# Output projection of a hybrid decoder layer: pools in another order, row statistics behind three accumulations, norms one tile later

## The chip, the core and the metric

One core of a Trainium2 chip runs the whole layer as one program. The metric is the device time of one execution in microseconds (us). TensorE is called PE, its weight loads PEld, VectorE DVE, ScalarE ACT, GpSimd POOL; SP is the queue that issues nearly all DMAs.

## What is computed

The reference, cut to the part that matters. `oa` and `ob` are the outputs of two groups of attention heads, 2048 positions by 512 columns each.

```python
mixed = jnp.concatenate([rmsnorm(oa, g_out_a[l]), rmsnorm(ob, g_out_b[l])], axis=-1)
x = x + jnp.einsum('bse,ed->bsd', mixed, w_o[l])
h = rmsnorm(x, g_ffn[l])
act = jax.nn.silu(jnp.einsum('bsd,df->bsf', h, w_gate[l])) * jnp.einsum('bsd,df->bsf', h, w_up[l])
x = x + jnp.einsum('bsf,fd->bsd', act, w_down[l])
return rmsnorm(x, g_final)
```

`rmsnorm(x, g)` divides each row by the root of its mean square and multiplies by `g`. `w_o` is 1024 by 1024, `w_gate` and `w_up` are 1024 by 2816, `w_down` is 2816 by 1024; all is float32. The layer before this part makes the input projection (`project`) and the two attentions (`MixerA`, `attend_b`).

## The kernel before

A float32 product is made of three matmuls of rounded operands: high by high, high by low, low by high. So each operand is split into a high half (a cast on ACT) and a low half (a subtraction on DVE or POOL), and a product over 512 columns of contraction takes 12 matmuls of 128x512.

**The projection** is `project_out`, lines 802 to 924. The 2048 rows are four tiles `t` of 512, and the contraction is two groups `g` of 512: `g` 0 for `oa`, 1 for `ob`. One call of `add(t, g)` (line 909) does one tile and one group:

- `prep_o` (833) loads four chunks of attention output (`ob`, 512 KB each, in two parts that are added at line 848) with their denominators `fb` (847), multiplies them (850 or 854, result `os_`), splits the result into the halves of `oT` (856 on ACT, 857 on DVE) and sums the squares over the four chunks (860 on ACT, 864 on DVE) into one buffer, `sacc`.
- Four matmuls of one column with a vector of ones (867, `pss`; a profile shows them as eight instructions) turn the squares into a sum per row; `rstd_of` (106) makes the reciprocal root of it: one DVE instruction (`ms_o`, 108) and one POOL power (`rs_o`, 110).
- `load_x` (827) fetches the tile's x into `xs`, with `g` 0 only.
- `outproj` (870) makes eight accumulations of 12 matmuls (881), 96 matmuls in all, and adds each to `xs` on DVE, scaled by `rs` (885, the eviction). On its first call for a group it loads and splits the weights `wo` (`load_wo`, 816; loads 821, casts 823, subtractions 824 on DVE for group 0 and on POOL for group 1).

`norm2(t)` (887) stores a finished tile (893), squares it on ACT (895), scales it in place on DVE (897), transposes it with 32 matmuls on PE (902), copies the transposes to `hst` on ACT (903) and stores them in DRAM as `hT` (905). `ffn_in` (927) loads `hT` of two tiles at a time again (`hraw`, 950), makes seven operands of it per chunk (A11, S2, S1, S3, A12, A22, S4; lines 953 to 972) and seven split weights (`wh`, `wl`, 977 and 979), and starts with `first_quads` (1043), whose first matmul is line 1050.

**What sets the order.** Python writes the program in the order of the calls, and a scheduler with a model of the machine then merges it into one list per engine and queue. Each engine runs its list in order. The calls are: `add(0,0)`, `add(1,0)`, `add(0,1)`, then for t = 1 to 3 `norm2(t-1)`, `add(t,1)`, `add(t+1,0)`, and `norm2(3)`.

**Buffers.** PSUM has eight banks, all in the pool `ps` with the one tag `mm`: accumulations, `pss` and transposes share them. SBUF pools are stacked from the foot in the order in which they are opened (lines 809 to 811, after `rw3` with its four load buffers of 16 KB together, sizes per partition): `c3` 4 KB (`gf`, the row of g_ffn), `s3` some 4, `op` 20, `wo30` 32, `slot` 48 (six buffers of `oT`, three groups), `x3` 32 (two tiles of `xs`), `hst` 16, `wo31` 32. Before this phase the same room belongs to the attention's pools, and after it to those of `ffn_in`: `g3` 12, `t3` 28, `a3` 112 (the operands, in the order of the list above, high half then low half), `whl3` 36 (the split weights). A tile waits for whatever used its room before (`reuse_waits="tile"`).

Of the kernel before, what the change touches and what calls it, by code (L numbers as in the profile page):

```python
# [13 lines left out]
ALU = mybir.AluOpType  # L14
# [11 lines left out]
NT = S // 512  # L26
# [79 lines left out]
def rstd_of(nc, pool, ss, n, width, half, name, bufs=2):  # L106
    ms = pool.tile([P, width], F32, tag="ms", name="ms_" + name, bufs=bufs)
    nc.vector.tensor_scalar(out=ms, in0=ss, scalar1=1.0 / n, scalar2=EPS, op0=ALU.mult, op1=ALU.add)  # L108
    rs = pool.tile([P, width], F32, tag="rs", name="rs_" + name, bufs=bufs)
    nc.gpsimd.tensor_tensor(out=rs, in0=ms, in1=half[:, :width], op=ALU.pow)  # L110
    return rs


def bcast_row(nc, dst, row):
    nc.sync.dma_start(dst, row.partition_broadcast(P))
# [669 lines left out]
def phase3(tc, consts, x, w_o, g_ffn, w_gate, w_up, w_down, g_final, out, sc):  # L785
    nc = tc.nc
    with ExitStack() as es:
        ps = es.enter_context(tc.tile_pool(name="ps3", bufs=8, space=PSUM, reuse_waits="tile"))
        rw = es.enter_context(tc.tile_pool(name="rw3", bufs=4, reuse_waits="tile"))
        project_out(tc, consts, ps, rw, x, w_o, g_ffn, sc)  # L790
        ffn_in(tc, ps, rw, w_gate, w_up, sc)
        ffn_out(tc, consts, ps, rw, w_down, g_final, out, sc)
# [9 lines left out]
def project_out(tc, consts, ps, rw, x, w_o, g_ffn, sc):  # L802

    nc = tc.nc
    ident, half, ones, gout = consts
    xr = x[0].rearrange("(i r) d -> r i d", r=16)
    wov = w_o[0].rearrange("(k p) n -> p k n", p=P)
    with ExitStack() as es:
        pool = lambda name, bufs: es.enter_context(tc.tile_pool(name=name, bufs=bufs, reuse_waits="tile"))
        cp, sp, op, wp0, slot, xp, hp, wp1 = (pool(n, b) for n, b in (  # L810
            ("c3", 1), ("s3", 2), ("op", 2), ("wo30", 1), ("slot", 6), ("x3", 2), ("hst", 2), ("wo31", 1)))
        wp = (wp0, wp1)
        gf = cp.tile([P, D], F32, name="gf")
        wo = {}

        def load_wo(g, hf):
            wh = wp[g].tile([P, 4, 512], F32R, tag=f"woh{g}{hf}", name=f"woh{g}{hf}")
            wl = wp[g].tile([P, 4, 512], F32R, tag=f"wol{g}{hf}", name=f"wol{g}{hf}")
            for u in range(2):
                raw = rw.tile([P, 2, 512], F32, tag="raw", name="wraw_o")  # L820
                nc.sync.dma_start(raw, wov[:, 4 * g + 2 * u:4 * g + 2 * u + 2, hf * 512:(hf + 1) * 512])
                ks = slice(2 * u, 2 * u + 2)
                nc.scalar.copy(wh[:, ks], raw)
                (nc.gpsimd if g else nc.vector).tensor_sub(wl[:, ks], raw, wh[:, ks].bitcast(F32))
            wo[g, hf] = (wh, wl)

        def load_x(t):
            xs = xp.tile([P, 4, D], F32, tag="xs", name=f"xs{t}")
            for i in range(4):
                nc.sync.dma_start(xs[:, i, :], xr[RES[4 * t + i]])  # L830
            return xs

        def prep_o(t, g):

            dma = nc.sync.dma_start
            oT = [slot.tile([P, 2, 2, 512], F32R, tag="slot", name="oT") for _ in range(2)]
            for k in range(4 * g, 4 * g + 4):
                ob = op.tile([P, 2, 512], F32, tag="ob", name="ob")
                os_ = op.tile([P, 512], F32, tag="os", name="os_")
                rows = slice((k % 4) * P, (k % 4 + 1) * P)  # L840
                if k < 4:
                    dma(ob, sc.oA[:, t, rows, :].rearrange("s p n -> p s n"))
                else:
                    dma(ob, sc.oB[:, rows, t * 512:(t + 1) * 512].rearrange("s p n -> p s n"))
                fb = op.tile([P, 512], F32, tag="fb", name="fb")
                for u in range(2):
                    dma(fb[u * 64:u * 64 + 64], (sc.fA[t, 2 * k + u] if k < 4 else sc.fB[k - 4, t, u]).partition_broadcast(64))
                nc.vector.tensor_add(ob[:, 0], ob[:, 0], ob[:, 1])
                if k < 4:
                    nc.vector.tensor_mul(os_.rearrange("p (r j a) -> p r j a", r=4, j=16),  # L850
                                         ob[:, 0].rearrange("p (j r a) -> p r j a", j=16, r=4),
                                         fb.rearrange("p (j r a) -> p r j a", j=16, r=4))
                else:
                    nc.vector.tensor_mul(os_, ob[:, 0], fb)
                hi, lo = oT[k % 4 // 2][:, k % 2, 0], oT[k % 4 // 2][:, k % 2, 1]
                nc.scalar.activation(hi, os_, AF.Copy, scale=gout[:, k:k + 1])
                nc.vector.scalar_tensor_tensor(lo, os_, gout[:, k:k + 1], hi.bitcast(F32),
                                               op0=ALU.mult, op1=ALU.subtract)
                sq = op.tile([P, 512], F32, tag="sq" if k % 4 else "sacc", name="sq3", bufs=1)
                nc.scalar.activation(sq, os_, AF.Square)  # L860
                if k % 4 == 0:
                    acc = sq
                else:
                    nc.vector.tensor_add(acc, acc, sq)
            pss = ps.tile([P, 4], F32, tag="mm", name="pss")
            for i in range(4):
                nc.tensor.matmul(pss[:, i:i + 1], acc[:, i * P:(i + 1) * P], ones, start=True, stop=True)
            return oT, rstd_of(nc, sp, pss, 512, 4, half, f"o{t}{g}")

        def outproj(xs, g, oT, rs):  # L870
            for hf in range(2):
                if (g, hf) not in wo:
                    load_wo(g, hf)
            for i in range(4):
                for hf in range(2):
                    wh, wl = wo[g, hf]
                    acc = ps.tile([P, 512], F32, tag="mm", name="acco")
                    n = 0
                    for kk in range(4):
                        for a, b in ((0, wh), (0, wl), (1, wh)):  # L880
                            nc.tensor.matmul(acc, oT[kk // 2][:, kk % 2, a, i * P:(i + 1) * P], b[:, kk, :],  # L881
                                             start=(n == 0), stop=(n == 11))
                            n += 1
                    xv = xs[:, i, hf * 512:(hf + 1) * 512]
                    nc.vector.scalar_tensor_tensor(xv, acc, rs[:, i:i + 1], xv, op0=ALU.mult, op1=ALU.add)

        def norm2(t, xs):
            hst = [hp.tile([P, 4, 512], F32, tag="hst", name="hst") for _ in range(2)]
            sq = sp.tile([P, D], F32, tag="sqr", name="sqr", bufs=1)
            for i in range(4):  # L890
                cols = slice(i * P, (i + 1) * P)
                h2 = xs[:, i, :]
                nc.sync.dma_start(sc.x1[t, :, i], h2)
                ss = sp.tile([P, 1], F32, tag="ssr", name="ssr")
                nc.scalar.activation(sq, h2, AF.Square, accum_out=ss)
                rs = rstd_of(nc, sp, ss, D, 1, half, f"f{t}_{i}")
                nc.vector.scalar_tensor_tensor(h2, h2, rs, gf, op0=ALU.mult, op1=ALU.mult)
                for kg in range(2):
                    pt = ps.tile([P, 4, P], F32, tag="mm", name="pt3")
                    for kk in range(4):  # L900
                        k = kg * 4 + kk
                        nc.tensor.transpose(pt[:, kk, :], h2[:, k * P:(k + 1) * P], ident)
                    nc.scalar.copy(hst[kg][:, :, cols], pt)
            for kg in range(2):
                nc.sync.dma_start(sc.hT[t, :, 4 * kg:4 * kg + 4, :], hst[kg])

        xs = {}

        def add(t, g):
            o = prep_o(t, g)  # L910
            if g == 0:
                xs[t] = load_x(t)
            outproj(xs[t], g, *o)

        add(0, 0)
        add(1, 0)
        bcast_row(nc, gf, g_ffn[0])
        add(0, 1)
        for t in range(1, NT):
            norm2(t - 1, xs[t - 1])  # L920
            add(t, 1)
            if t + 1 < NT:
                add(t + 1, 0)
        norm2(NT - 1, xs[NT - 1])


# [295 lines left out]
```

## Time and profile before

| | us |
|---|---|
| median of three runs (2484.49 to 2489.96) | 2489.6 |
| the profiled execution | 2490.19 |
| its span, first to last instruction | 2488.4 |
| PE busy in the span | 2373.2 (95%) |
| DVE, ACT, POOL busy | 1444.7, 1029.5, 457.9 |
| the projection's first and last accumulating matmul | 888.3, 1111.7 |
| mean granted TensorE clock, of full speed | 0.974 |

The span lies inside the execution's time; some 2 us are around it. Busy time of PE overlaps, as matmuls are pipelined, so a stretch is read by when instructions start and by what ended the idle time before them. The granted clock has two levels, 1.2 and 2.4 GHz; a mean between them says for how much of a stretch each was granted.

### The profile page before, as it was taken

The numbers are of one execution on the slowest core, as the hardware profiler recorded it, in microseconds if no ns is written. First come the engines' busy times: TensorE is split into PE (matmuls) and PEld (weight loads), VectorE is DVE, ScalarE is ACT, GpSimd is POOL, SyncE is SP. The second block draws the span as 40 slices with busy tenths as digits, with TensorE's granted clock in tenths as the row PEclk, the third lists the DMA queues.
The fourth block names the chain that finished last, engine by engine and source line by source line (L and its number), as shares of the span: only waits on it lengthen the run. The fifth ranks groups of instructions, "written<-read, shape, count | busy, mean of one in ns | idle before, by whom it ended". The sixth has DMA issues, their size and how long they took to land. (4 is left out here: it accounts for less than half of the span.)

```text
span 2488.4 us, 33691 instructions
## 1 busy us (share of the span) xinstructions
PE 2373.2 (95%) x12029; PEld 2016.7 (81%) x12029; DVE 1444.7 (58%) x2969; ACT 1029.5 (41%) x2361; POOL 457.9 (18%) x431
## 2 busy tenths in 40 slices
PE   7999999989999878997999999899999999999998
PEld 7987788878999767775888888688888878888886
DVE  5335544457999766659655665965566433434342
ACT  5323355454888933335323333432332232423241
POOL 2311211111111010112110110311011051414140
PEclk9999999997999988998999999999999999999999
DMA  7666666668896886724222222422222163636361
GB/s 220 209 191 204 166 187 168 154 182 209 216 224 166 217 245 218 248 103 148 93 85 78 92 85 68 134 87 85 85 85 85 64 234 131 239 119 237 123 232 60
DMA packets 250136, 384.27 MB, mean 154 GB/s; under 512 B 19680, under 2 KB 148320, under 8 KB 244464
## 3 DMA queue, kind: packets, MB, share of 16 engines
q1 hardware_dynamic: 244784, 367.03, 49.0%
q0 software_dynamic: 4896, 14.75, 1.9%
q8 instruction: 95, 1.56, 0.3%
q14 instruction: 73, 0.60, 0.1%
q10 hardware_dynamic: 288, 0.33, 0.0%
HBM read 263.43 MB, written 118.62 MB: 154 GB/s over the span
## 5 line engine op out<-in xcount | busy, mean ns | idle before, releaser
L1136 PE MATMUL dn<-wh_d,act 128*128 128x512 f32 x1408 | 434.9, 390 | 2.4 <-ACT act L1116 2.3
L1136 PEld LDWEIGHTS dn<-wh_d,act 128*128 128x128 f32 x1408 | 264.9, 188 | 58.4 <-ACT act L1116 2.7
L1127 DVE TENSOR_TENSOR wl_d<-wraw_d,wh_d 128x1024 fp32r<-128x1024 f32 x88 | 138.3, 1578 | 272.1 <-ACT wh_d L1125 272.1
L1136 PE MATMUL dn<-wl_d,act 128*128 128x512 f32 x704 | 274.4, 390 | 0.0
L1084 POOL TENSOR_TENSOR c<-c,c 128x512 f32<-128x512 f32 x66 | 104.8, 1589 | 713.5 <-DVE c L1030 524.6
L977 ACT CAST wh<-T 128x512 fp32r<-128x512 f32 x176 | 108.7, 622 | 257.3 <-PE Yg L1012 71.7
L468 DVE TENSOR_TENSOR hl<-pt,hl 128x512 fp32r<-128x512 f32 (+1 forms) x224 | 145.2, 657 | 80.2 <-ACT hl L467 79.6
L443 ACT ACTIVATE p<-t,m 128x256 f32<-128x256 f32 (+1 forms) x384 | 176.8, 477 | 25.9 <-DVE m L668 25.9
L169 PE MATMUL acc<-hh,wh 128*128 128x512 f32 x416 | 170.1, 409 | 0.7 <-DVE vt L239 0.7
L169 PE MATMUL acc<-hh,wl 128*128 128x512 f32 x416 | 170.4, 410 | 0.0
L169 PE MATMUL acc<-hl,wh 128*128 128x512 f32 x416 | 170.0, 409 | 0.0
L1117 POOL TENSOR_TENSOR act<-actr,act 128x512 fp32r<-128x512 f32 x88 | 122.7, 1414 | 256.9 <-ACT act L1116 256.8
L881 PE MATMUL acco<-woh,oT 128*128 128x512 f32 x512 | 166.2, 404 | 0.0
L1125 ACT CAST wh_d<-wraw_d 128x1024 fp32r<-128x1024 f32 x88 | 92.1, 1050 | 166.8 <-PE dn L1136 145.2
L1136 PEld LDWEIGHTS dn<-wl_d,act 128*128 128x128 f32 x704 | 132.5, 188 | 27.5
L486 PE MATMUL o<-hl,v 128*128 128x128 f32 (+1 forms) x816 | 142.5, 295 | 7.1 <-DVE hl L468 6.1
L421 PE MATMUL s<-k,q 128*128 128x256 f32 (+1 forms) x768 | 131.9, 310 | 15.9 <-DVE hl L468 7.1
L467 ACT CAST hl<-pt 128x512 fp32r<-128x512 f32 (+1 forms) x224 | 124.7, 566 | 45.5 <-PE pt L462 45.1
L979 DVE TENSOR_TENSOR wl<-T,wh 128x512 fp32r<-128x512 f32 x176 | 122.7, 701 | 32.9 <-ACT wh L977 32.6
L462 PE MATMUL pt<-ident,p 128*128 128x128 f32 x848 | 134.2, 280 | 2.4 <-ACT p L443 1.6
L421 PEld LDWEIGHTS s<-k,q 128*128 128x128 f32 x768 | 111.1, 212 | 23.2 <-DVE nma L558 7.3
L486 PEld LDWEIGHTS o<-hl,v 128*128 128x128 f32 x816 | 112.2, 194 | 11.7 <-DVE hl L468 9.6
(453 smaller groups left out, 5520.4 us busy)
## 6 DMA issues: line engine op xcount, KB each, us to landing
wraw_d<-in_w_down_dram SPq DMA_DIRECT2D x88, 512.0 KB
wraw_g<-in_w_gate_dram SPq DMA_DIRECT2D x44, 512.0 KB
wraw_u<-in_w_up_dram SPq DMA_DIRECT2D x44, 512.0 KB
actr<-actS SPq DMA_DIRECT2D x44, 512.0 KB
actS<-c SPq DMA_DIRECT2D x68, 256.0 KB
k<-kB SPq DMA_DIRECT2D x32, 512.0 KB
xt<-in_x_dram SPq DMA_DIRECT2D x16, 512.0 KB
qA<-hia SPq DMA_DIRECT2D x32, 256.0 KB
```

The lines of the kernel that those rows point to most:

```text
L169: nc.tensor.matmul(acc, a[:, k, :], mv, start=(n == 0), stop=(n == 3 * KC - 1))
L421: nc.tensor.matmul(s[:, i, :n], b["q"], b["k"][m], start=(m == 0), stop=(m == 1))
L443: nc.scalar.activation(b["pv"](p[:, i, :n]), b["tv"](b["t"]), AF.Exp, scale=-1.0, bias=nm[:, c:c + 1], accum_out=l[:, c:c + 1])
L462: nc.tensor.transpose(pt[:, sl, :], p[:, i, hfn * P:(hfn + 1) * P], ident)
L467: nc.scalar.copy(hi, pt[:, a:z, :])
L468: nc.vector.tensor_sub(lo, pt[:, a:z, :], hi.bitcast(F32))
L486: nc.tensor.matmul(out, v[:, vi, :], mov, start=(first and n == 1), stop=(last and n == 2 * len(jobs)))
L881: nc.tensor.matmul(acc, oT[kk // 2][:, kk % 2, a, i * P:(i + 1) * P], b[:, kk, :], start=(n == 0), stop=(n == 11))
L979: nc.vector.tensor_sub(lo, src, hi.bitcast(F32))
L1117: nc.gpsimd.tensor_sub(a[:, 1], raw[:, u], a[:, 0].bitcast(F32))
L1127: nc.vector.tensor_sub(wl, raw, wh.bitcast(F32))
L1136: nc.tensor.matmul(acc[i], acts[kk][:, a, i * P:(i + 1) * P], w[kk // 2][b][:, kk % 2, :], start=(kk == 0 and n == 0), stop=(kk == NF - 1 ...
```

## The change

The pools are opened in another order, `op` and `wo30` first and `c3` and `s3` last. `prep_o` returns the summed squares instead of their reciprocal root, and `outproj` makes that root after its third accumulation (`group_rstd`); the three finished accumulations are evicted then, each later one as it ends. The calls at the end now run tile by tile, each norm after the next tile's two groups.

```diff
--- before.py
+++ after.py
@@ -807,8 +807,8 @@
     wov = w_o[0].rearrange("(k p) n -> p k n", p=P)
     with ExitStack() as es:
         pool = lambda name, bufs: es.enter_context(tc.tile_pool(name=name, bufs=bufs, reuse_waits="tile"))
-        cp, sp, op, wp0, slot, xp, hp, wp1 = (pool(n, b) for n, b in (
-            ("c3", 1), ("s3", 2), ("op", 2), ("wo30", 1), ("slot", 6), ("x3", 2), ("hst", 2), ("wo31", 1)))
+        op, wp0, slot, xp, hp, wp1, cp, sp = (pool(n, b) for n, b in (
+            ("op", 2), ("wo30", 1), ("slot", 6), ("x3", 2), ("hst", 2), ("wo31", 1), ("c3", 1), ("s3", 2)))
         wp = (wp0, wp1)
         gf = cp.tile([P, D], F32, name="gf")
         wo = {}
@@ -862,15 +862,19 @@
                     acc = sq
                 else:
                     nc.vector.tensor_add(acc, acc, sq)
+            return oT, acc
+
+        def group_rstd(t, g, acc):
             pss = ps.tile([P, 4], F32, tag="mm", name="pss")
             for i in range(4):
                 nc.tensor.matmul(pss[:, i:i + 1], acc[:, i * P:(i + 1) * P], ones, start=True, stop=True)
-            return oT, rstd_of(nc, sp, pss, 512, 4, half, f"o{t}{g}")
-
-        def outproj(xs, g, oT, rs):
+            return rstd_of(nc, sp, pss, 512, 4, half, f"o{t}{g}")
+
+        def outproj(t, xs, g, oT, sq):
             for hf in range(2):
                 if (g, hf) not in wo:
                     load_wo(g, hf)
+            accs = []
             for i in range(4):
                 for hf in range(2):
                     wh, wl = wo[g, hf]
@@ -881,8 +885,14 @@
                             nc.tensor.matmul(acc, oT[kk // 2][:, kk % 2, a, i * P:(i + 1) * P], b[:, kk, :],
                                              start=(n == 0), stop=(n == 11))
                             n += 1
-                    xv = xs[:, i, hf * 512:(hf + 1) * 512]
-                    nc.vector.scalar_tensor_tensor(xv, acc, rs[:, i:i + 1], xv, op0=ALU.mult, op1=ALU.add)
+                    accs.append((i, hf, acc))
+
+                    if len(accs) == 3:
+                        rs = group_rstd(t, g, sq)
+                    if len(accs) >= 3:
+                        for i_, hf_, acc in accs if len(accs) == 3 else accs[-1:]:
+                            xv = xs[:, i_, hf_ * 512:(hf_ + 1) * 512]
+                            nc.vector.scalar_tensor_tensor(xv, acc, rs[:, i_:i_ + 1], xv, op0=ALU.mult, op1=ALU.add)
 
         def norm2(t, xs):
             hst = [hp.tile([P, 4, 512], F32, tag="hst", name="hst") for _ in range(2)]
@@ -910,17 +920,18 @@
             o = prep_o(t, g)
             if g == 0:
                 xs[t] = load_x(t)
-            outproj(xs[t], g, *o)
+            outproj(t, xs[t], g, *o)
 
         add(0, 0)
         add(1, 0)
         bcast_row(nc, gf, g_ffn[0])
         add(0, 1)
-        for t in range(1, NT):
+        add(1, 1)
+        norm2(0, xs[0])
+        for t in range(2, NT):
+            add(t, 0)
+            add(t, 1)
             norm2(t - 1, xs[t - 1])
-            add(t, 1)
-            if t + 1 < NT:
-                add(t + 1, 0)
         norm2(NT - 1, xs[NT - 1])
```

How the instruction lists change at three places:

PE at the end of the attention, before. `o` and `pf` are the last matmuls of the attention and a transpose of its denominators.

```order
L486 MATMUL o<-hl,v_1_9937 128x2x4x32 x5
L486 MATMUL o<-hl,v_1_9937 128x4x32 x2
L681 MATMUL pf<-ident,rcs 32x128
L867 MATMUL pss<-ones_83,sq_10288 128x1 x4
L881 MATMUL acco<-woh_10343,oT 128x512
L881 MATMUL acco<-wol_10344,oT 128x512
```

And now, the same place:

```order
L486 MATMUL o<-hl,v_1_9937 128x2x4x32 x5
L486 MATMUL o<-hl,v_1_9937 128x4x32 x2
L681 MATMUL pf<-ident,rcs 32x128
L885 MATMUL acco<-woh_10334,oT 128x512
L885 MATMUL acco<-wol_10335,oT 128x512
```

The sums of squares have left this place; they follow 36 matmuls later, behind the third accumulation, and so in each of the eight groups.

SP in the attention's second to last stretch, before. `wraw_o` are the weights of the projection, `gf` is g_ffn, `v_0` and `v_1` belong to the last attention head.

```order
L821 DMA wraw_o<-in_w_o_dram 128x2x512 x3
L842 DMA ob<-oA 128x2x512
L847 DMA fb<-fA 64x512 x2
L821 DMA wraw_o<-in_w_o_dram 128x2x512
L115 DMA gf<-in_g_ffn_dram 128x1024
L842 DMA ob<-oA 128x2x512
L847 DMA fb<-fA 64x512 x2
L613 DMA v_0_9935<-vR 128x16x128
L617 DMA v_1_9937<-vR 32x16x128 x3
```

And now:

```order
L821 DMA wraw_o<-in_w_o_dram 128x2x512 x3
L842 DMA ob<-oA 128x2x512
L847 DMA fb<-fA 64x512 x2
L821 DMA wraw_o<-in_w_o_dram 128x2x512
L842 DMA ob<-oA 128x2x512
L847 DMA fb<-fA 64x512 x2
L821 DMA wraw_o<-in_w_o_dram 128x2x512 x3
L613 DMA v_0_9935<-vR 128x16x128
L617 DMA v_1_9937<-vR 32x16x128 x2
```

Three loads of the second group's weights stand ahead of the last head's v, and `gf` has left. On ACT the four casts of the first group's weights (line 823) stood behind the last cast of the attention; now they stand among its exponentials, some 40 to 55 rows earlier, and the four DVE subtractions (824) with them.

ACT at the end of the phase, before. `hst` are the copies of the last tile's transposes, `wh` the first weights of the FFN.

```order
L903 COPY hst<-pt_12055 128x4x128
L903 COPY hst<-pt_12061 128x4x128
L977 CAST wh<-wraw_g 128x512
L977 CAST wh<-T_12099 128x512
L977 CAST wh<-T_12097 128x512
L977 CAST wh<-T_12109 128x512
L977 CAST wh<-wraw_g 128x512
L977 CAST wh<-T_12119 128x512
L977 CAST wh<-wraw_g 128x512
L955 CAST A11h<-hraw 128x512
```

And now:

```order
L988 CAST wh<-T_12119 128x512
L988 CAST wh<-wraw_g 128x512
L913 COPY hst<-pt_11995 128x4x128
L913 COPY hst<-pt_12015 128x4x128
L913 COPY hst<-pt_12035 128x4x128
L913 COPY hst<-pt_12055 128x4x128
L913 COPY hst<-pt_12001 128x4x128
L913 COPY hst<-pt_12021 128x4x128
L913 COPY hst<-pt_12041 128x4x128
L913 COPY hst<-pt_12061 128x4x128
L966 CAST A11h<-hraw 128x512
```

The seven weight casts stand ahead of the last tile's eight copies now. Ahead of those casts stand the eight copies of the tile before it, whose 32 transposes PE makes right before the last tile's 32.

## Rows read from the trace of the kernel before

**Rows 1.** The page's 40 slices of the span: PE busy, granted clock, in tenths.

```profile
PE   7999999989999878997999999899999999999998
PEclk9999999997999988998999999999999999999999
```

**Rows 2.** Stretches: length, busy of PE, PEld, DVE, ACT, POOL, clock, DMA share, GB/s.

```profile
836.00:842.00 6.00, 5.49 (x27) 5.30 (x27) 5.80 (x17) 2.55 (x8) 0.00 (x0) 0.50 1.05 367
876.00:894.00 18.00, 8.03 (x27) 6.43 (x26) 12.32 (x19) 6.59 (x10) 1.04 (x1) 0.62 1.00 305
...
1112.00:1130.00 18.00, 4.84 (x35) 4.20 (x34) 6.99 (x12) 10.44 (x21) 0.54 (x1) 0.68 0.45 175
```

**Rows 3.** PE in order of time: start, us, engine, line, count [idle before, what ended it].

```profile
875.42 0.80 PE L486 MATMUL o<-hl,v 128*128 128x256 f32 x5 [0.24 <-DVE hl L468]
881.79 0.37 PE L681 MATMUL pf<-ident,rcs 128*32 128x128 f32 x1 [5.57 <-DVE rcs L678]
886.56 1.87 PE L867 MATMUL pss<-ones,sq 128*128 128x1 f32 x8 [4.40 <-DVE sq L864]
...
893.70 0.40 PE L881 MATMUL acco<-wol,oT 128*128 128x512 f32 x1
...
912.32 0.39 PE L881 MATMUL acco<-woh,oT 128*128 128x512 f32 x1
917.36 1.87 PE L867 MATMUL pss<-ones,sq 128*128 128x1 f32 x8 [4.64 <-DVE sq L864]
...
924.47 0.40 PE L881 MATMUL acco<-wol,oT 128*128 128x512 f32 x1
...
943.32 0.95 PE L867 MATMUL pss<-ones,sq 128*128 128x1 f32 x8
...
966.03 1.03 PE L902 MATMUL pt<-ident,xs 128*128 128x128 f32 x8
...
985.85 0.40 PE L881 MATMUL acco<-wol,oT 128*128 128x512 f32 x1
...
1028.11 3.66 PE L902 MATMUL pt<-ident,xs 128*128 128x128 f32 x32
1037.39 1.87 PE L867 MATMUL pss<-ones,sq 128*128 128x1 f32 x8 [5.62 <-DVE xs L885]
...
1043.78 0.62 PE L881 MATMUL acco<-woh,oT 128*128 128x512 f32 x2
...
1111.97 2.78 PE L902 MATMUL pt<-ident,xs 128*128 128x128 f32 x24
...
1129.01 0.79 PE L1050 MATMUL FA<-A11h,wh 128*128 128x512 f32 x1 [10.94 <-ACT A11h L955]
```

**Rows 4.** DVE in order of time, the same columns.

```profile
877.33 1.22 DVE L824 TENSOR_TENSOR wol<-wraw_o,woh 128x1024 fp32r<-128x1024 f32 x1
...
890.51 0.69 DVE L848 TENSOR_TENSOR ob<-ob 128x512 f32<-128x512 f32 x1 [1.88 <-DMA ob<-oA]
...
907.46 3.85 DVE L848 TENSOR_TENSOR ob<-ob 128x512 f32<-128x512 f32 x1 [4.84 <-DMA ob<-oA]
...
1035.98 0.69 DVE L848 TENSOR_TENSOR ob<-ob 128x512 f32<-128x512 f32 x1 [5.15 <-DMA ob<-oB]
```

**Rows 5.** ACT in order of time, the same columns.

```profile
839.96 0.63 ACT L860 ACTIVATE sq<-os__10291 128x512 f32<-128x512 f32 x1 [2.65 <-DVE os__10291 L850]
...
874.67 3.87 ACT L823 CAST woh<-wraw_o 128x1024 fp32r<-128x1024 f32 x4
...
1029.95 3.98 ACT L903 COPY hst<-pt 128x512 f32<-128x512 f32 x8
...
1124.70 0.62 ACT L977 CAST wh<-wraw_g 128x512 fp32r<-128x512 f32 x1 [5.96 <-DMA hT<-hst]
```

**Rows 6.** SP's queue in order of time: issue of the last tile's two stores.

```profile
1118.28 0.81 SPq L905 DMA_DIRECT2D hT<-hst  x2
```

**Rows 7.** POOL in order of time, the same columns.

```profile
903.56 7.19 POOL L824 TENSOR_TENSOR wol<-wraw_o,woh 128x1024 fp32r<-128x1024 f32 x3
```

## The prediction

> **What bounds the kernel now.** I read the page's 40 slices first: TensorE (PE) is at 9 in most of them; of the few that are lower, four lie close together (62.2 us a slice): 8, 7, 8 in the 14th to 16th (809 to 995 us) and 7 in the 19th (1120 to 1182), and the granted clock is at 8 in three of these [rows 1]. That is the output projection and its two borders, and the whole change lies there. Next I read the stretches around the drops. Over 876 to 894 us PE is busy 8.03 of 18 us at a mean granted clock of 0.62, over 1112 to 1130 4.84 of 18 us at 0.68 [rows 2]. Then PE's own order of time with what ended each idle stretch [rows 3]. The reader is to see a pattern there. Matmuls of 512 columns start 0.227 us apart at the full 2.4 GHz: from 893.70 (the 14th of a group of 96) to 912.32 (the 96th) are 82 steps in 18.62 us. Every long stall is followed by matmuls and sums of squares at 1.2 GHz (eight pss matmuls take 1.87 us at 917.36, 0.95 at 943.32), until the clock comes back some 6 to 7 us after PE resumed.
>
> I price a place as the time from its last full-speed matmul to the first full-speed one after it, less the same work at full rate (0.227 us a matmul, 0.8 us the eight pss instructions, 3.7 us the 32 transposes of a tile, as at 1028.11). All from [rows 3]:
> - a, border to the attention: 876.2 (875.42 + 0.80) to 893.70 is 17.5 us; work 0.4 + 0.8 + 13 x 0.227 = 4.2; loss **13.3**.
> - b, second group: 912.55 to 924.47 is 11.9; work 0.8 + 13 x 0.227 = 3.8; loss **8.1**.
> - c, first norm: 966.03 to 985.85 is 19.8; work 3.7 + 0.8 + 10 x 0.227 = 6.8; loss **13.0**.
> - d, second norm: 1028.11 to 1043.78 is 15.7; work 3.7 + 0.8 + 11 x 0.227 = 7.0; loss **8.7**.
> - e, border to the FFN: from 1111.97 to the first FFN matmul at 1129.01 are 17.0 us, with 3.7 of transposes in them.
>
> So 43 us are lost at a to d and about 13 at e. The third and sixth to eighth groups, whose sums of squares were ready, show nothing of it: at 943.32 PE runs on.
>
> **The change part by part.**
>
> *Sums of squares behind three accumulations.* The same eight pss instructions per group, but PE no longer needs them to begin. At 886.56 and 917.36 it sat 4.40 and 4.64 us for the last sum (DVE sq); now it needs only the oT halves. The three accumulations (36 x 0.227 = 8.2 us) cover the chain of sums. If that cover is gone, the old wait returns at its old price. New waits: three PSUM banks and one for pss are held until the reciprocal root is there. Eight banks minus these four leave four accumulations, 4 x 12 x 0.227 = 10.9 us, before PE would stand. The chain is one DVE instruction, one POOL power and a DVE eviction, some 3 us when DVE is free. The single accumulator of squares is held 8.2 us longer, so the next group's third and fourth chunks are prepared behind it; 13.6 us of its group then remain for them. I cost both at nothing.
>
> *Norms between other tiles' projections.* In c and d, PE stood since a tile's norm followed its own last eviction directly: the transposes waited for ms_f and xs, and at 1037.39 for DVE evictions (5.62 us) that stood in DVE's order behind an addition waiting 5.15 us for its load [rows 4]. Now 21.8 us of another tile's group lie between. The transposes of tiles 0 and 1 find their rows ready; only the fourth row's normalisation still comes near the end, and 24 transposes (2.8 us) run ahead of it. I take c and d whole: 13.0 + 8.7 = **21.7**. Bounds: nothing, if another wait takes each place, to 21.7; I take the upper end since PE's queue holds nothing there any more that is late. What could be late next is the load of the next tile's x: it waits for these transposes, and 512 KB pieces of it share the queue with the 2 MB stores of hT. The first eviction that needs it now comes 8.2 us later than before, which covers it.
>
> *Pool order, at a.* With op and wo30 at the foot, the first weights no longer wait for the attention's late buffers. Their four ACT casts (3.87 us at 874.67) and four DVE subtractions move from behind the attention into it. Two of those subtractions, of 1.22 us each, stood before the last reciprocal, which releases pf at 881.79 [rows 3, 4]: pf comes 2.4 us sooner after the attention's end. All four stood before the last oT half. So PE would start its projection at about 880 instead of 888.4 (886.56 + 1.87), if the attention ended as now. It will not: the casts now stand among exponentials on ACT. One cast fits into the 2.65 us that ACT idled before 839.96; the other three, 0.97 us each, push a full engine by **2.9** us [rows 5]. On SP, three more 512 KB weight loads go ahead of the last head's v loads, one (g_ffn) leaves: 1.05 MB more in a queue that was full at 367 GB/s over 836 to 842 [rows 2], 2.9 us. Both delay the same stages at the same time, so I count 2.9 once (bounds 0 and 5.8). What is left of a: an idle stretch of 881.79 - 2.4 - 876.2 = 3.2, 2.9 of delay, a slow clock once more (about eleven matmuls at twice their time, 11 x 0.227 = 2.5) and, as an estimate, 0.5 of waiting for the last oT half: 9.1 of 13.3. Gain **4** (1 to 9; the upper end if the clock does not fall at all).
>
> Behind it stands a page: by the Trainium skill, DMA: Bandwidth & Descriptors (Queues, rings and completion order), descriptors on an engine are consumed in ring order. By that the v loads cannot overtake the weights, and the sum would lose another 2.9 if the two delays add.
>
> *Second group, b.* Its third chunk was late because a DVE addition at 907.46 waited for its load and then took 3.85 us, not 0.69 as at 890.51 [rows 4]. Ahead of that load now stand 2.1 MB of second-half weights fewer and 0.5 MB of g_ffn more: about 1.6 MB at 305 GB/s (876 to 894 [rows 2]), 5 us sooner, against a start 2.9 us later and a PE that asks 4.5 us earlier. I leave 1.5 us of stall: gain **6.5** (0 to 8.1).
>
> *Border e.* Let E be PE's last projection matmul. Before, FFN weight casts stood until 1124.70 for the store of hst [rows 5], since the new pools lay over hst. Now those pools lie over wo31, free at E, and the seven casts run early. But tile 2's norm moved to the end too: its eight copies (4.0 us, as at 1029.95) end about E + 6; tile 3's copies need the same two hst buffers, so they wait for that store, 6.4 us (1118.28 to 1124.70 [rows 5, 6]): E + 12.7, plus four copies and one cast: first FFN matmul near E + 15.4 instead of E + 17.0. After it, operands A22 and S4 lie over hst and wait for the last store, about E + 21, while weights and the second chunk are further ahead than before. Gain **2** (-5 to 6).
>
> Sum: 4 + 6.5 + 21.7 + 2 = 34.2. The profiled execution took 2490.2 us (0.6 above the median 2489.6): 2490.2 - 34.2 = **2456**.
>
> **The rivals.**
> - *The first 50 us give nothing back* (a 1, b 0): ACT and DMA are both full at the attention's end, and the slow DVE addition of 3.85 us ran while POOL subtracted weights, three in 7.19 us from 903.56 [rows 7]. POOL's four subtractions now come some 15 us earlier, onto the second group's preparation; a DVE addition under them took up to 3.2 us more (3.85 - 0.69), and two or three of them caught so cost 6 to 9 us of the lead that DVE has over PE. Against it: PE has 22 us of the first group to hide that. 2456 + 3 + 6.5 = 2465.5. A page stands behind it: by the Trainium skill, GPSIMD Engine Reference (Specifications), GpSimd shares its SBUF interfaces with VectorE and contends with instructions of two SBUF inputs; 3.85 against 0.69 agrees.
> - *The tail turns worse*: the two norms meet in two hst buffers, and the last operands wait for two stores in a row. At the lower bound of e, -5 instead of 2: 2463.
> - *Half of c and d stays*, as DVE's order still puts evictions behind preparation that waits for loads (5.62 us at 1037.39 was that): 2456 + 11 = 2467.
> - *Slower*: the held banks. If pss, POOL's power and the first eviction take over 10.9 us, PE stands in every group. All 34.2 us are eaten from 10.9 + 34.2/8 = 15.2 us on; at 16.5 us the run takes about 2500. For it: DVE waits of 5 us stand in its order. Against: 5 + 3 is under 10.9, and no group's chain was near 15.
>
> That the new order isn't what the diff says is excluded: the instruction order shows both moves.
>
> **How the numbers follow.** Forecast 0.52, first rival 0.20, tail 0.15, half of c and d 0.08, slower 0.03, other 0.02. The forecast's own range is 2446 to 2463; first rival with the tail gives 2473. Range **2444 to 2474**. A measurement tells 0.3% (7.5 us) from no change: below 2482 is faster. All cases but the last two are there, save part of their combinations: faster 0.92, same 0.05, slower 0.03.
>
> **What would show it.** Right: PE's first acco some 5 us earlier, followed directly by 36 matmuls; no idle over 2 us between the groups and no half clock from about 890 to E; transposes of 3.7 us at three places, 7.4 at the last; E near 1076 (1112 - 32.2 - 3.7). Wrong: PE waiting on DVE xs or rs in the fourth to eighth accumulation (banks), on oT in the second group, on v in the attention, or on S4 for over 6 us in the FFN's first products. If E comes 30 us earlier but the end doesn't, the FFN's start took it back.

## The result, and the profile after

The changed kernel takes 2462.1 us (median of 4 runs, 2457.23 to 2466.92) against 2487.99 for the kernel before: a ratio of 0.9897, 95% interval 0.9874 to 0.9921, 25.9 us faster. The prediction said 2456.0, range 2444 to 2474. The profiled execution took 2461.1 us, its span is 2459.3. The slices on the profile's page of the changed kernel (62 us each), which answer to [rows 1]:

```profile
PE   7999999998999898989999999899999999999998
PEclk9999999998999899999999999999999999999999
```

The granted clock is at 9 in all slices of the projection and of the FFN's start now (the 15th to the 19th); three of these stood at 8. The 14th, still in the attention, went from 9 to 8. TensorE in order of time in the changed kernel (start, us, line, count, idle before and what ended it), beside [rows 3]:

```profile
876.22 0.27 PE L681 MATMUL pf<-ident,rcs 128*32 128x128 f32 x1 [3.30 <-DVE rcs L678]
876.24 0.48 PE L885 MATMUL acco<-woh,oT 128*128 128x512 f32 x1
...
886.15 0.95 PE L870 MATMUL pss<-ones,sq 128*128 128x1 f32 x8
...
927.11 0.73 PE L885 MATMUL acco<-woh,oT 128*128 128x512 f32 x2 [0.97 <-DVE oT L857]
...
970.18 1.03 PE L912 MATMUL pt<-ident,xs 128*128 128x128 f32 x8
974.44 1.09 PE L912 MATMUL pt<-ident,xs 128*128 128x128 f32 x8 [3.22 <-DVE xs L907]
980.42 1.97 PE L912 MATMUL pt<-ident,xs 128*128 128x128 f32 x8 [4.89 <-DVE xs L907]
982.94 1.97 PE L912 MATMUL pt<-ident,xs 128*128 128x128 f32 x8 [0.55 <-DVE xs L907]
...
1035.68 1.10 PE L912 MATMUL pt<-ident,xs 128*128 128x128 f32 x8 [1.42 <-DVE xs L907]
...
1096.83 0.80 PE L1061 MATMUL FA<-A11h,wh 128*128 128x512 f32 x1 [4.62 <-ACT A11h L966]
...
1104.29 0.79 PE L1061 MATMUL FA<-A11l,wh 128*128 128x512 f32 x1 [5.39 <-DVE A11l L967]
```

The first projection matmul follows `pf` at once, and no sum of squares is waited for. But the first norm still stands in the chain: 3.22, 4.89 and 0.55 us of idle time, followed by matmuls at half clock.

**Not all of the 29.1 us between the two spans is the change.** At 780 us, far ahead of the first instruction that the change moves, the profiled execution is already 7.0 us ahead. It was 0.2 us behind at 560 us and 7.0 ahead at 600: the granted clock of TensorE in that stretch differs from execution to execution. The stretch from 580 to 600 us (length, PE busy with its count, clock, DMA share, GB/s) of the kernel before, of the changed one, and of the changed one in a second profile (e11):

```profile
580.00:600.00 20.00, 18.71 (x85) 0.59 1.08 233
```

```profile
580.00:600.00 20.00, 17.14 (x116) 1.00 1.07 236
```

```profile
580.00:600.00 20.00, 19.00 (x85) 0.54 1.03 231
```

In all 14 profiles the time at 780 us lay between 2.2 us behind the profile of before and 7.7 ahead, whatever the kernel. So below I compare places, not spans, by the prediction's own method: the time from the last full-speed matmul to the first one after it, less the work at full rate. "Delay" is how much later the attention ended, against the same execution's time at 780 us; columns a to d are losses in us; the last column is the gain from the last matmul of the projection to the 200th of the FFN, the transposes of tile 2 counted in.

| kernel | median us | delay | a | b | c | d | gain at e |
|---|---|---|---|---|---|---|---|
| before | 2488.0 | 0 | 13.3 | 8.1 | 13.0 | 8.7 | 0 |
| changed | 2462.1 | 3.7 | 5.1 | 1.3 | 11.6 | 2.0 | 2.7 |
| changed again (e11) | 2464.0 | 2.8 | 5.4 | 0.2 | 12.1 | 2.0 | 2.7 |
| calls alone (e2) | 2477.6 | 0 | 13.0 | 4.5 | 11.0 | 2.5 | -1.3 |
| pools alone (e3) | 2473.2 | 3.8 | 8.0 | 7.3 | 12.7 | 0 | 0.4 |
| sums alone (e7) | 2477.2 | -0.3 | 8.1 | 6.3 | 12.4 | 5.3 | -0.5 |
| without the calls (e10) | 2468.0 | 3.1 | 5.5 | 0 | 15.2 | 5.3 | 0.7 |
| own statistics buffers (e1) | 2457.3 | 2.5 | 5.1 | 2.1 | 10.0 | 0.4 | 4.0 |
| the same, third ob buffer (e6) | 2454.6 | 1.3 | 7.1 | 2.7 | 5.9 | 0 | 4.6 |
| e1 without tile 2's loads (e9) | 2453.7 | 2.5 | 6.2 | 0.1 | 1.2 | 1.3 | 4.2 |

For the changed kernel: -3.7 + 8.2 + 6.8 + 1.4 + 6.7 + 2.7 = 22.1, and with the 7.0 ahead 29.1, the difference of the spans. For its second profile, 23.3 - 2.2 = 21.1 against 21.5. Two profiles of one kernel differ by 1.1 us at a place (b of the changed kernel) and 1.2 (c of e6, repeated as e12), so a smaller difference between two rows of the table says nothing.

### The profile page after: what moved, and what is told of

It is laid out like the page before. It is cut to its first block, busy times and chain, and to the rows that moved or that the text cites. A ratio compares the mean times of both kernels' runs of the same rounds, so it can differ in the third digit from the quotient of the medians.

```text
span 2459.3 us, 33676 instructions
## 1 busy us (share of the span) xinstructions
PE 2357.3 (96%) x12029; PEld 1999.6 (81%) x12029; DVE 1441.7 (59%) x2969; ACT 1028.2 (42%) x2361; POOL 460.6 (19%) x431
## 5 line engine op out<-in xcount | busy, mean ns | idle before, releaser
L421 PE MATMUL s<-k,q 128*128 128x256 f32 (+1 forms) x768 | 122.1, 290 | 18.5 <-DMA k<-kB 8.7
L421 PEld LDWEIGHTS s<-k,q 128*128 128x128 f32 x768 | 100.8, 192 | 26.4 <-DVE nma L558 7.1
```

The costliest lines, as they stand in the source:

```text
L421: nc.tensor.matmul(s[:, i, :n], b["q"], b["k"][m], start=(m == 0), stop=(m == 1))
```

## The experiments

The first norm (c) was the open question, 11.6 us where I had expected none. VectorE in order of time around it, changed kernel:

```profile
963.65 0.69 DVE L848 TENSOR_TENSOR ob<-ob 128x512 f32<-128x512 f32 x1 [3.93 <-DMA ob<-oB]
964.25 0.15 DVE L108 TENSOR_SCALAR ms_o<-pss 128x4 f32<-128x4 f32 x1
964.33 0.14 DVE L108 TENSOR_SCALAR ms_f<-ssr 128x1 f32<-128x1 f32 x1
...
968.02 1.27 DVE L907 SCALAR_TENSOR_TENSOR xs<-xs,rs_f,gf 128x1024 f32<-128x1024 f32 x1
...
973.11 1.28 DVE L907 SCALAR_TENSOR_TENSOR xs<-xs,rs_f,gf 128x1024 f32<-128x1024 f32 x1
...
977.82 0.69 DVE L848 TENSOR_TENSOR ob<-ob 128x512 f32<-128x512 f32 x1 [0.85 <-DMA ob<-oB]
...
979.09 1.28 DVE L907 SCALAR_TENSOR_TENSOR xs<-xs,rs_f,gf 128x1024 f32<-128x1024 f32 x1
...
981.60 1.28 DVE L907 SCALAR_TENSOR_TENSOR xs<-xs,rs_f,gf 128x1024 f32<-128x1024 f32 x1
```

Each stretch of transposes starts some 0.05 us after a scaling (line 907) ends: 973.11 + 1.28 = 974.39 and PE at 974.44, then 980.37 and 980.42, 982.88 and 982.94. Two things hold the scalings. The first row's statistic, `ms_f`, whose squares ACT had ready at 945.98, waits until 964.33, right behind `ms_o` of the next group, with which it shares the two buffers of `ms` and `rs`. And `ms_o`, whose `pss` were done at 956.6, stands behind an addition that waited 3.93 us for its load. That gave two theories: the shared buffers, or DVE's order behind loads.

**e1: own buffers for the norm's statistics.**

```diff
-                ss = sp.tile([P, 1], F32, tag="ssr", name="ssr")
+                ss = sp.tile([P, 1], F32, tag="ssr", name="ssr", bufs=4)
...
-                rs = rstd_of(nc, sp, ss, D, 1, half, f"f{t}_{i}")
+                rs = rstd_of(nc, sp, ss, D, 1, half, f"f{t}_{i}", 4, "n")
```

(the last argument is appended to the tags `ms` and `rs`.)

> The changed kernel, but the row statistics of the norms get buffers of their own (four deep) instead of sharing the two-deep ms and rs buffers with the groups. Theory: the first norm still stalls PE because its first statistic must wait, in buffer order, for that of the next group, which the change moved behind 36 matmuls. Then the 32 transposes of tile 0 take under 6 us instead of 14.7, those of tile 1 under 5 instead of 5.8, and the time falls by 9 to 13 us, to about 2451. Rival: DVE's order, with additions that wait for loads, holds the scaling back whatever the buffers: the 32 transposes stay over 11 us and the time within 4 us of the changed kernel's.

Measured 2457.3 us, ratio to before 0.987 (0.9855 to 0.9884). Tile 0's transposes took 13.2 us: the theory of the buffers failed as the cause of c. Its statistics did come early, with the last scaling over at 966, and the second norm (d 0.4) and the border to the FFN (4.0) came out better. What held the transposes then, PE of e1:

```profile
977.59 1.11 PE L912 MATMUL pt<-ident,xs 128*128 128x128 f32 x4 [2.47 <-DVE xs L895]
982.30 1.12 PE L912 MATMUL pt<-ident,xs 128*128 128x128 f32 x4 [3.60 <-DVE xs L895]
```

and DVE of e1:

```profile
967.77 0.69 DVE L848 TENSOR_TENSOR ob<-ob 128x512 f32<-128x512 f32 x1 [1.80 <-DMA ob<-oB]
968.38 0.15 DVE L108 TENSOR_SCALAR ms_o<-pss 128x4 f32<-128x4 f32 x1
...
976.79 0.75 DVE L895 SCALAR_TENSOR_TENSOR xs<-acco,rs_o,xs 128x512 f32<-128x512 f32 x1
...
981.51 0.74 DVE L895 SCALAR_TENSOR_TENSOR xs<-acco,rs_o,xs 128x512 f32<-128x512 f32 x1
```

The four transposes of a bank start at the end of an eviction of an accumulation (977.54 and 977.59, 982.25 and 982.30): so they wait for a PSUM bank. The statistic `ms_o` of that group came 8.8 us after its `pss` (done at 959.6), again behind a load. So the wait is the rival's, only that PSUM banks carry it to PE in place of the scalings. Not all of it is additions: ahead of the eviction at 981.51 stands a scaling (979.70) that waited 0.84 us for the store of the same rows of x.

**e2: the order of the calls alone** (`add(1,1)`, `norm2(0)`, then `add(t,0)`, `add(t,1)`, `norm2(t-1)`, in the kernel before).

> The kernel before with the order of the calls alone. Theory of the shared buffers: the sums of squares still stand first in each group, so the statistic of group (1,1) comes 8 us sooner than in the changed kernel and the norm of tile 0 is not held; its transposes lose under 4 us (13.0 with their slow clock before, 11.6 in the changed kernel), those of tile 1 under 2; the border of the attention and the second group lose 13 and 8 as before; time about 2474 (2468 to 2480). Rival (DVE's order behind loads): the transposes of tile 0 lose over 9, time 2481 or more.

Measured 2477.6 us, ratio 0.9956 (0.9938 to 0.9973). The time lies where the theory of the buffers had put it, but for other reasons: the sums come first in each group here, and c still loses 11.0, as the rival said, so the statistics' place isn't the cause; the second group lost only 4.5 where 8 was expected. Its transposes, too, start at the ends of evictions (line 885): PE of e2

```profile
985.94 0.73 PE L902 MATMUL pt<-ident,xs 128*128 128x128 f32 x4 [3.52 <-DVE xs L885]
...
991.10 1.11 PE L902 MATMUL pt<-ident,xs 128*128 128x128 f32 x4 [2.51 <-DVE xs L885]
```

and just ahead of the evictions that end at 985.88 and 991.05 DVE of e2 has additions that waited for their loads:

```profile
983.93 0.69 DVE L848 TENSOR_TENSOR ob<-ob 128x512 f32<-128x512 f32 x1 [2.22 <-DMA ob<-oB]
...
989.69 0.69 DVE L848 TENSOR_TENSOR ob<-ob 128x512 f32<-128x512 f32 x1 [2.27 <-DMA ob<-oA]
```

**e3: the order of the pools alone.**

> The kernel before with the order of the pools alone. The attention ends 3 to 4 us later (weight casts among the exponentials); pf waits 3.3 instead of 5.6; PE still waits for the sums of squares, which come about 5 us sooner after the attention's end; so 1 to 2 us net at that border. Second group: 0 to 6 of its 8.1, if its loads were the late thing. First and second norm as before (13.0 and 8.7). FFN's start: weights split early, 2 to 4 us. Together 2481 (2474 to 2486). If the pool order alone gave over 15 us, the deferred sums would be worth nothing.

Measured 2473.2 us, ratio 0.993 (0.9907 to 0.9954), more than expected. The border came as expected: 3.8 of delay for 5.3 of gain. But the second norm lost nothing, which I had not expected. DVE of e3, to be read beside the last line of [rows 4]:

```profile
1024.77 0.74 DVE L885 SCALAR_TENSOR_TENSOR xs<-acco,rs_o,xs 128x512 f32<-128x512 f32 x1
1029.23 0.69 DVE L848 TENSOR_TENSOR ob<-ob 128x512 f32<-128x512 f32 x1 [3.72 <-DMA ob<-oB]
```

The addition waits for its load here too, 3.72 us, but the evictions that PE needed stand ahead of it now. By these rows the 8.7 us at d hung on one place in DVE's order.

**e4: norm of tile 2 between the two groups of tile 3.**

```diff
             add(t, 0)
+            if t > 2:
+                norm2(t - 1, xs[t - 1])
             add(t, 1)
-            norm2(t - 1, xs[t - 1])
+            if t == 2:
+                norm2(t - 1, xs[t - 1])
```

> The changed kernel with the norm of tile 2 called between the two groups of tile 3 instead of behind them. Theory: the two norms in a row cost at the border to the FFN. Its 32 transposes go ahead of the last group, the last matmul of the projection comes 3.7 us later, and the first FFN matmul about 9 us after it instead of 14.7; 2 to 4 us net, about 2459. Rival: the FFN's first products are bound by the load of the last tile's hT, so what PE starts earlier it waits later (5.4 us now, then 8): no difference.

Measured 2461.95 us, ratio 0.9903 (0.9877 to 0.9929): no difference, as the rival said. The FFN did start 9.9 us after the projection's last matmul instead of 14.7, and waited then. PE of e4:

```profile
1091.80 0.80 PE L1064 MATMUL FA<-A11h,wh 128*128 128x512 f32 x1 [2.55 <-ACT A11h L969]
...
1102.43 0.80 PE L1064 MATMUL FS<-S1l,wh 128*128 128x512 f32 x1 [5.14 <-DVE S1l L970]
```

By the table's measure it gains 0.8 us at e where the changed kernel gains 2.7. In which order the operands' loads and splits bound the FFN's start was not tried.

**e5 and e6: a third buffer for the loaded chunks**, alone (e5) and with e1's buffers (e6).

```diff
-                ob = op.tile([P, 2, 512], F32, tag="ob", name="ob")
+                ob = op.tile([P, 2, 512], F32, tag="ob", name="ob", bufs=3)
...
-            sq = sp.tile([P, D], F32, tag="sqr", name="sqr", bufs=1)
+            sq = sp.tile([P, D], mybir.dt.bfloat16, tag="sqr", name="sqr", bufs=1)
```

> The changed kernel with three buffers instead of two for the loaded chunks ob (the room comes from the norm's unused squares, now bfloat16). Theory after e1 and e2: what keeps PE at the first norm is DVE's order, where evictions and scalings stand behind additions that wait 1 to 4 us for their loads, as a load is only issued when one of two buffers is free. Then additions wait under 1 us between 950 and 990 us, and the 32 transposes of tile 0 take under 9 us instead of 14.7 (the shared statistics buffers still hold the norm's first row until the group's sums): 5 to 7 us less, about 2456. Rival: the loads are slow in themselves, beside the stores of x; then a third buffer changes under 2 us.

> e1 (own buffers for the norm's statistics) and e5 (third ob buffer) together. Theory: in e1 the transposes started each right after an eviction, so PSUM banks held them, and the evictions stood behind a load; with neither left, the 32 transposes of tile 0 take under 6 us (13.2 in e1), those of tile 1 about 4; 8 to 11 us under the changed kernel, about 2452. Rival: banks are short in any case, since the sums now hold four of eight until the reciprocal root; then tile 0's transposes stay over 10.

e5: 2460.2 us, ratio 0.9905 (0.988 to 0.993), with c at 10.8 and 12.7 us of transposes, nearer the rival: additions still waited 4.25 and 2.61 us before 960.74 and 964.04. e6: 2454.6, ratio 0.9887 (0.9859 to 0.9915); c fell to 5.9, d to nothing. Either cure alone moved c by under 2 us, both by 5.7. The 9.3 us of transposes in e6 lie between the theory's 6 and the rival's 10. What was left, PE of e6:

```profile
973.03 2.34 PE L912 MATMUL pt<-ident,xs 128*128 128x128 f32 x20
979.06 0.66 PE L912 MATMUL pt<-ident,xs 128*128 128x128 f32 x4 [3.69 <-DVE xs L895]
```

and DVE of e6, where an addition that waited stands ahead of the eviction that ends at 979.00 (another had waited 2.60 us before 965.97):

```profile
975.13 0.69 DVE L848 TENSOR_TENSOR ob<-ob 128x512 f32<-128x512 f32 x1 [0.99 <-DMA ob<-oB]
...
978.26 0.74 DVE L895 SCALAR_TENSOR_TENSOR xs<-acco,rs_o,xs 128x512 f32<-128x512 f32 x1
```

The third buffer moves the pools above it by 4 KB, and with it the first weights' casts went back to the attention's end (869.8 to 872.7 us in e5, and likewise in e6); the delay was 0.1 us in e5, and the loss at a 8.5. Against the changed kernel that is 3.4 more loss at a and 3.6 less delay: once the sums are deferred, the early weights are worth nothing there.

**e7: the deferred sums alone.**

> The kernel before with the deferred sums alone. At the attention's end no delay; pf waits 5.6 as before, then the projection starts when the last oT half is there, 4 to 5 us sooner than before; second group gains about 6 of 8.1. First and second norm as before or 1 to 3 worse, as evictions come later. FFN's start as before. Together 2478 (2473 to 2484). Rival (the held banks cost what the covered sums give): 2486 or more.

Measured 2477.2 us (10 runs), ratio 0.9965 (0.9949 to 0.9982). The border gained 5.2 as expected; the second group only 1.8 of the 6, and the norms came out better, not worse (0.6 and 3.4). In the second group an oT half was late, PE of e7:

```profile
913.31 0.79 PE L885 MATMUL acco<-woh,oT 128*128 128x512 f32 x1 [3.30 <-ACT oT L856]
```

**e8: the casts of the first weights on POOL.**

```diff
-                nc.scalar.copy(wh[:, ks], raw)
+                (nc.scalar.copy if g else nc.gpsimd.tensor_copy)(wh[:, ks], raw)
```

> The changed kernel with the four casts of the first group's weights on POOL instead of ACT. In the changed kernel the attention ends 3.7 us later against its own start than before. If the four casts among ACT's exponentials (0.95 us each) are the cause, the delay falls under 1 us and the time by 2 to 4 us, to about 2459, unless POOL brings the weights later than the first accumulation needs them. If the three earlier weight loads ahead of v are the cause, the delay stays at 3 to 4 us.

Measured 2462.7 us, ratio 0.9917 (0.9892 to 0.9942), and the attention still ended 3.4 us late, which is what I had set down for the weight loads ahead of v. But in the changed kernel the delay of ACT's exponentials grows by 0.8 us over the first two casts together and by 0.95 over each of the other two, to 2.7. ACT of the changed kernel:

```profile
837.18 1.04 ACT L823 CAST woh<-wraw_o 128x1024 fp32r<-128x1024 f32 x1
...
843.76 1.05 ACT L823 CAST woh<-wraw_o 128x1024 fp32r<-128x1024 f32 x1
```

Without them, ACT of e8 stands for a chunk of the first group, 4.34 us where [rows 5] had 2.65:

```profile
837.17 0.63 ACT L860 ACTIVATE sq<-os__10291 128x512 f32<-128x512 f32 x1 [4.34 <-DVE os__10291 L850]
```

Moving the casts changed the order of the loads as well, so it isn't shown that the casts alone cost the 3.7; e5, with the casts at the attention's end and a delay of 0.1, shows that the early weights, loads and casts together, do. Which of the two it is stays open.

**e9: e1 without the loads of tile 2.**

```diff
-                if k < 4:
+                if t == 2:
+                    nc.gpsimd.memset(ob, 1.0)
+                elif k < 4:
```

> e1 with the chunk loads of tile 2 left out (a fill by POOL stands in their place, so tile 2's rows are computed from ones). These are the loads for which DVE's additions wait while tile 0's norm is due. Theory (evictions and scalings stand behind additions that wait for loads, and the PSUM banks with them): no such wait between 950 and 990 us, and tile 0's 32 transposes take under 6 us (13.2 in e1, 9.3 in e6). Rival (four of eight banks held until the reciprocal root, or DVE's own work, set it): they stay over 9.

PE of e9, one execution of 2453.7 us (it leaves out loads, so its tile 2 is not the layer's):

```profile
976.19 2.94 PE L914 MATMUL pt<-ident,xs 128*128 128x128 f32 x24
980.17 1.09 PE L914 MATMUL pt<-ident,xs 128*128 128x128 f32 x8 [1.05 <-ACT hst L915]
```

The transposes take 5.1 us and c loses 1.2, against 13.2 and 10.0 in e1. DVE does the same additions, most of them a few places earlier in its order than in e1, and waits for no load between 942 and 990 us. With that the cause of c in e1 is shown: additions that wait for loads, in DVE's order ahead of scalings and evictions. Four held banks, the sums held longer and DVE's own work, all of which e9 keeps, do not stall PE for more than the 1.2. For the changed kernel itself the same cause is read from its rows (the 3.93 us before 963.65) and from e6, where a third buffer for the loads helped once the statistics had their own; it was not run without the loads and with the shared buffers.

**e10: the changed kernel with the calls as before.**

> The changed kernel with the calls in the order of before (pools and sums changed). Theory: the calls add little to the other two, since the first norm stalls in either order and the pools' order alone already takes away the second norm's stall: first norm 12 to 14 us lost, second 0 to 3, and 2 to 5 us slower than the changed kernel, 2464 to 2467. Rival (my prediction's): the calls are worth over half of 21.7, so 2473 or more.

Measured 2468.0 us, ratio 0.9927 (0.9906 to 0.9949): 4.0 us over the changed kernel on the same chip. Beside the other two parts the calls are worth 3.6 at c, 3.3 at d and 2.0 at e, by the table. The time came as the theory said, the places didn't quite: the first norm lost 15.2 (12 to 14 expected) and the second 5.3 (0 to 3). The pools' order takes the stall at d away when it is alone (e3), but not beside the deferred sums. By places e10 gains 14.7 where the changed kernel gains 22.1 and 23.3; that is more than the 4.0 between the medians, whose runs scatter by 4 and 12 us, so the size is open. First stall of its first norm, PE of e10:

```profile
950.19 1.97 PE L912 MATMUL pt<-ident,xs 128*128 128x128 f32 x8 [4.50 <-DVE xs L907]
```

**e11 and e12: the changed kernel again, and e6 again, on one chip.**

> The changed kernel again, beside the next run on the same chip: 2457 to 2467, with the first norm's transposes at 14 to 15 us. The time up to the second attention should differ from the first profile's by up to 7 us, since the granted clock of 558 to 600 us differed so between all profiles.

> e6 again, for the comparison with the changed kernel on one chip: 6 to 10 us faster than it. If it is within 3 us, the version is no better than the changed kernel by what a measurement can tell.

e11: 2464.0 us (2456.39 to 2468.7), ratio 0.9907 (0.9887 to 0.9926), tile 0's transposes 15.1 us. e12: 2456.7 (2451.99 to 2460.16), ratio 0.9877 (0.9857 to 0.9898), c at 7.1, d 0, so c is 5.0 below e11's. The version with own statistics buffers and a third chunk buffer is 7.2 us faster by the medians, and e6 was 7.5 faster than the first measurement of the changed kernel; the intervals of the two ratios overlap in part, while c and d are smaller in both of its profiles. It isn't shown to be faster than e1, which has the statistics buffers alone: e1's ratio of 0.987 (0.9855 to 0.9884) lies no higher.

## Why the prediction was right or wrong

- **The total lay in the range, in part by luck.** 34.2 us were forecast and 25.9 measured between the medians. By places, the change is worth 22.1 and 23.3; the rest I put down to the clock ahead of it, and both values lie within the ratio's interval (19.7 to 31.3 us). The range reached up to 2474 for the first rival together with the tail; neither came, and the 13.6 us missing at c and d fell into that room.
- **a, gain 4: right.** Measured 8.2 less 3.7, so 4.5 (7.9 less 2.8 in e11). The delay was given as 2.9 and the idle stretch ahead of `pf` as 3.2 (3.30). The sum was right, but I had put it down to the pools' order; e7 and e5 show that the deferred sums pay at this border, and that the early weights gain about what they delay. By the rule cited from the Trainium skill, DMA: Bandwidth & Descriptors (Queues, rings and completion order), that descriptors on an engine are consumed in ring order, the earlier weight loads could have added another 2.9; the 2.5 to 3.8 of all profiles with early weights and casts on ACT show no such sum.
- **b, gain 6.5: right in size.** 6.8 and 7.9. But I had priced it by the loads that come sooner, and e3, which has them, gains 0.8. The deferred sums alone give 1.8 (e7); the two together give it (8.1 in e10).
- **c and d, "I take c and d whole: 13.0 + 8.7 = 21.7": wrong.** 1.4 + 6.7 = 8.1; most of d came, hardly anything of c. The step that failed is "PE's queue holds nothing there any more that is late". The transposes stand later in PE's queue, but the scalings stand later in DVE's as well, behind the next group's statistic and behind additions that wait for loads. I had read just that wait at 1035.98 [rows 4] and taken it for a matter of one place. My third rival named the mechanism with a chance of 0.08; 13.6 of the 21.7 stayed where it said 11. The prediction's signs of being right failed here: PE idled 3.22 and 4.89 us and then ran at half clock, tile 0's transposes took 14.7 us and tile 1's 5.8 for 3.7 each, and the last projection matmul started at 1081.86, with the 7.0 of lead in it, for 1076.
- **The parts are not additive.** Alone, by places, pools give 11.7, sums 10.8, calls 10.8 us, 33.3 together, close to my 34.2; all three give 22.1. Each alone already takes 3.4 to 8.7 of the same 8.7 at d. I priced each place once, but as if only one edit served it.
- **e, gain 2: right**, 2.7. The FFN's first matmul came 14.7 us after E (1082.10 to 1096.83), forecast 15.4. With tile 2's transposes counted in that is 6.0 sooner than before; 2.7 of it were left at the FFN's steady rhythm, the rest went into the 5.39 us for A11l.
- **The first rival fell.** a and b gave back what I said, though DVE was slowed as it feared: an addition and a product took 2.92 and 2.77 us (883.86 and 886.82) while POOL's four subtractions ran from 879.13 for 9.91 us, against 0.69 otherwise. This agrees with the rule that GpSimd shares its SBUF interfaces with VectorE, named from the Trainium skill, GPSIMD Engine Reference (Specifications). The cost was hidden, as PE had the whole first group to do.
- **The slower rival's bound was nearly reached.** In the fourth group the first eviction ended some 11 us after `pss` began (955.63 to 966.7), the bound being 10.9 of accumulations; these ran on without a wait. What late evictions hold up are the transposes behind them, as e1 shows.

## What to carry to other kernels

Before pricing a step that is moved past other work as "free", look in the order of the engine that feeds it for instructions that wait for loads: what stands behind them is late whatever it needs, and a later place in the consumer's queue mends it only in part (the new order of the calls took 3.6 of 15.2 us at c, e10 against the changed kernel). Small buffers with one tag tie unrelated chains together in program order; give a row statistic its own. And edits that each cure the same stall must not be added up.

## What was not expected of the hardware

The granted clock between 560 and 600 us came back at different times in executions of the same kernel: over 580 to 600 us it was 1.00 in one profile of the changed kernel and 0.54 in the other. The times at 780 us lie up to 9.8 us apart in the 14 profiles, and all that follows moves with them. Differences of a few us between single executions of this program are therefore read from the place itself, not from the span.
